# A hybrid decoder layer in fp32: the feed-forward products by one level of Strassen, with block sums kept in DRAM

## The chip, the core and the metric

The kernel runs on one core of a Trainium2 chip. The core has TensorE (matmul), VectorE, ScalarE, GpSimd and SyncE, each with its own instruction queue taken in order, an on-chip memory (SBUF) of 128 partitions, eight PSUM banks of 128 x 512 fp32 that TensorE writes, and 16 DMA engines that move data from and to DRAM. The metric is the device time of one execution in microseconds, as the median of several runs.

## What is computed

One decoder layer for 1024 tokens with 1024 channels: a modulated RMS norm, one input projection into gated DeltaNet heads and sliding-window attention heads, an output projection with a gated residual, then a second modulated norm and a SwiGLU feed-forward part, again with a gated residual. All of it is fp32. The change concerns the feed-forward part:

```python
D_FF = ((8 * D_MODEL // 3 + 255) // 256) * 256        # 2816
...
h2 = rms_norm(x, norm2_w[l]) * (1.0 + scale2) + shift2
ffn = (jax.nn.silu(h2 @ w_gate[l]) * (h2 @ w_up[l])) @ w_down[l]
x = x + gate2 * ffn
```

## The kernel before

Activations lie with channels on the partitions and tokens along the row: `h2` is eight blocks of 128 channels, `x1` the residual in eight blocks, each in two halves (`hf`) of 512 tokens. A matmul takes a 128x128 block of weights and 512 tokens. TensorE multiplies operands of reduced width in one pass, so each fp32 operand is split into a high and a low part (`split`: ScalarE copies the high part, GpSimd or VectorE subtracts to get the low one), and each product takes three passes, high x high, high x low and low x high (`mm3`). A unit (`unit`) is the three passes over all `KT` = 8 blocks of the inner dimension into one PSUM bank.

Weights come by `wunit`: a DMA of 512 KB on SyncE's queue into a raw tile, then `split` with GpSimd's subtraction. Pool `wp` holds two raw tiles and two split ones, so weights are prepared about one unit ahead.

The last stages are these. `out_proj(0)` and `out_proj(1)` multiply the mixed heads by `w_out`, one half of the tokens each, and update `x1` and a sum of squares. `norm2_gen(hf)` makes the row of reciprocal norms (a few matmuls, a chain of small VectorE steps in `rstd`, transposes in `rstd_row`) and then the modulated `h2` in high and low parts. The generator of the first half runs between the units of `out_proj(1)`, that of the second half between the first units of the feed-forward part.

The feed-forward part goes over the 22 blocks of 128 of the 2816 inner channels in four chunks (6, 6, 6, 4). For each block it runs four units (gate and up, two halves), takes SiLU from PSUM on ScalarE, multiplies on VectorE, and splits the result. After each chunk, eight output blocks by two halves are multiplied with `w_down` over the blocks of the chunk and added to `x1` from PSUM (line 1327). After the last chunk `x1` is stored.

The order of TensorE's instructions is that of the program text (`manual_schedule`). The order on the other engines, DMA issues on SyncE's queue included, is set ahead of time by a planner that takes instructions by their place in the text when they are ready on a timeline it works out. Tiles of one `tag` in a pool share `bufs` buffers; a new tile waits until the users of the buffer's last one are done. Tags that matter: `s16` in pool `p16` (four buffers of 16 KB a partition: `h`, `mixed`, then `act`), `s8` in `p8` (four of 8 KB), `scr` (three of 2 KB).

## Time and profile before

| | |
|---|---|
| runs | 1372.16 us median of 3 (1367.86 to 1377.49) |
| the profiled execution, its span | 1368.4 us |
| TensorE matmul busy | 1274.6 us, 93% of the span |
| VectorE, GpSimd, ScalarE busy | 653.0, 468.7, 436.1 us |
| moved by DMA | 144.12 MB, mean 105 GB/s |
| feed-forward part | from 641.8 us to the end |

Matmuls are pipelined, so the busy time of one overlaps that of the next, and the time from start to start is what counts. The shares are means over stages that differ much: in the first half of the span VectorE is busy most of the time, in the feed-forward part it is mostly idle. A wait is put down to the engine that released it last.

### The profile page before, as it was taken

What the parts mean: (1) busy time and instruction counts of PE and PEld (TensorE: products, weight loads), DVE (VectorE), ACT (ScalarE), POOL (GpSimd) and SP (SyncE); (2) the same over time, 40 slices, a digit from 0 to 9 for tenths busy, and PEclk for the clock granted to TensorE, in tenths of its full rate; (3) what the DMA queues carried; (4) which work ended last, traced back from release to release, by engine and by line L of the source; (5) the groups of instructions that cost most, each with busy time, mean ns of one, the idle gap of its engine ahead of it and who ended that gap; (6) DMA issues with size and microseconds to landing.
All of it is one profiled execution on the core that took longest, in us unless ns stands there. A gap on an engine that the chain in (4) does not pass through costs nothing.

```text
span 1368.4 us, 18093 instructions
## 1 busy us (share of the span) xinstructions
PE 1274.6 (93%) x7106; PEld 1053.8 (77%) x7106; DVE 653.0 (48%) x1315; ACT 436.1 (32%) x787; POOL 468.7 (34%) x295
## 2 busy tenths in 40 slices
PE   6878697896999999999999999999999999999998
PEld 5767576684787777777788888888888888888887
DVE  7989899889425776666611211212211221211122
ACT  3464454422426775334411101112101211111210
POOL 5566445435333443455312122222222221222221
PEclk7878898998998999999999999999999999999999
DMA  8627378483758764323111111111111111111113
GB/s 325 220 83 273 122 165 237 131 257 104 217 154 148 139 131 134 101 87 101 46 45 43 35 46 62 47 47 54 35 53 59 46 46 44 44 59 56 39 60 117
DMA packets 111620, 144.12 MB, mean 105 GB/s; under 512 B 36528, under 2 KB 77744, under 8 KB 111408
## 3 DMA queue, kind: packets, MB, share of 16 engines
q1 hardware_dynamic: 101936, 134.58, 32.1%
q0 software_dynamic: 9600, 8.39, 3.7%
...
HBM read 118.14 MB, written 24.77 MB: 104 GB/s over the span
## 4 chain that ended last, share of the span: by engine, by line
PE 53%; ACT 1%; DVE 1%; POOL 0%; issue 0%; POOLq 0%; ACTq 0%
PE ps_d L203 6%; PE ps_d L202 6%; PE ps_d L201 6%; PE ps_u L201 6%; PE ps_u L203 6%; PE ps_u L202 6%; PE ps_g L202 6%; PE ps_g L203 6%; PE ps_g L201 6%; PE ps_o L203 0%; PE ps_o L202 0%; PE ps_o L201 0%; DVE xn L319 0%; DVE h L321 0%; ACT w_o L181 0%; POOL xn L323 0%
## 5 line engine op out<-in xcount | busy, mean ns | idle before, releaser
L1319 DVE TENSOR_TENSOR av<-ps_u,av 128x512 f32<-128x512 f32 x44 | 30.4, 692 | 333.4 <-PE ps_u L203 330.2
L201 PE MATMUL ps_d<-act,w_d 128*128 128x512 f32 x352 | 136.9, 389 | 0.0
L202 PE MATMUL ps_d<-act,w_d 128*128 128x512 f32 x352 | 136.9, 389 | 0.0
L203 PE MATMUL ps_d<-act,w_d 128*128 128x512 f32 x352 | 136.9, 389 | 0.0
L1327 DVE SCALAR_TENSOR_TENSOR x<-ps_d,modc,x 128x512 f32<-128x512 f32 x64 | 48.1, 751 | 181.6 <-PE ps_d L203 181.5
L1318 ACT ACTIVATE av<-ps_g 128x512 f32<-128x512 f32 x44 | 26.2, 598 | 181.3 <-PE ps_g L203 181.2
L182 DVE TENSOR_TENSOR act<-av,act 128x512 fp32r<-128x512 f32 x44 | 66.8, 1518 | 35.5 <-ACT act L181 35.5
L201 PEld LDWEIGHTS ps_d<-act,w_d 128*128 128x128 f32 x352 | 66.1, 188 | 13.7
L202 PEld LDWEIGHTS ps_d<-act,w_d 128*128 128x128 f32 x352 | 66.1, 188 | 13.7
L203 PEld LDWEIGHTS ps_d<-act,w_d 128*128 128x128 f32 x352 | 66.1, 188 | 13.7
L202 PE MATMUL ps_g<-h2l,w_g 128*128 128x512 f32 x168 | 65.6, 390 | 1.7 <-DVE h2l L326 1.7
L201 PE MATMUL ps_g<-h2h,w_g 128*128 128x512 f32 x168 | 65.5, 390 | 0.6 <-ACT h2h L324 0.6
L201 PE MATMUL ps_u<-h,w_u 128*128 128x512 f32 x168 | 65.5, 390 | 0.0
L203 PE MATMUL ps_g<-h2h,w_g 128*128 128x512 f32 x168 | 65.4, 389 | 0.0
L203 PE MATMUL ps_u<-h,w_u 128*128 128x512 f32 x168 | 65.4, 389 | 0.0
L202 PE MATMUL ps_u<-h,w_u 128*128 128x512 f32 x168 | 65.4, 389 | 0.0
L201 PE MATMUL ps_g<-h,w_g 128*128 128x512 f32 x168 | 65.4, 389 | 0.0
L202 PE MATMUL ps_g<-h,w_g 128*128 128x512 f32 x168 | 65.4, 389 | 0.0
L203 PE MATMUL ps_g<-h,w_g 128*128 128x512 f32 x168 | 65.4, 389 | 0.0
L201 PE MATMUL ps_u<-h2h,w_u 128*128 128x512 f32 x168 | 65.4, 389 | 0.0
L202 PE MATMUL ps_u<-h2l,w_u 128*128 128x512 f32 x168 | 65.4, 389 | 0.0
L203 PE MATMUL ps_u<-h2h,w_u 128*128 128x512 f32 x168 | 65.4, 389 | 0.0
...
## 6 DMA issues: line engine op xcount, KB each, us to landing
ada<-in_ada_dram SPq DMA_DIRECT2D x48, 512.0 KB, 5.3
xt<-in_xT_dram SPq DMA_DIRECT2D x16, 256.0 KB, 5.1
AQ<-aq SPq DMA_DIRECT2D x16, 256.0 KB, 4.1
KQ<-kq SPq DMA_DIRECT2D x4, 1024.0 KB, 6.3
kvq<-KQ SPq DMA_DIRECT2D x8, 512.0 KB, 5.6
aqb<-AQ SPq DMA_DIRECT2D x8, 512.0 KB, 6.0
qb<-QS POOLq DMA_DIRECT2D x16, 256.0 KB, 8.4
x<-in_xT_dram SPq DMA_DIRECT2D x16, 256.0 KB, 3.3
```

What stands on the lines that cost most here:

```text
L182: last = eng.tensor_tensor(out=r(lo), in0=src, in1=hi, op=ALU.subtract)
L201: pe.matmul(out, lhsT=r(lhs[0]), rhs=r(rhs[0]), start=first, stop=False)
L202: pe.matmul(out, lhsT=r(lhs[0]), rhs=r(rhs[1]), start=False, stop=False)
L203: pe.matmul(out, lhsT=r(lhs[1]), rhs=r(rhs[0]), start=False, stop=last)
L1318: act.activation(out=av, in_=pss[0, hf], func=AF.Silu)
L1319: dve.tensor_tensor(out=av, in0=pss[1, hf], in1=av, op=ALU.mult)
L1327: dve.scalar_tensor_tensor(out=x, in0=ps, scalar=modc[:, 40 + dt:41 + dt], in1=x, op0=ALU.mult, op1=ALU.add)
```

## The change

Gate, up and down products are each computed by one level of Strassen's method in Winograd's form. An operand is cut into 2 x 2 blocks; sums and differences of blocks (S1 to S4 of the weights, T1 to T4 of the activations) are formed, seven products of half size take the place of eight, and the results are added up (U2, U3 and so on). The 22 blocks of inner channels go in 11 pairs `p`; the halves are the even and the odd block of a pair, the first and second four channel blocks, and the first and second half of the tokens.

Sweep 1 runs over the pairs with two products (A11 B11 and A12 B21) for gate and up; the first is copied to DRAM (`XD`), and their sum gives the first quarter of the activations (`AD[:, p, 0]`). Sweep 2 runs over the pairs again with the other five products, adds them up with what `XD` holds, and stores six more blocks or block sums of the activations (`AD[:, p, 1:7]`). In two of the five, a bank that VectorE has read is accumulated on again by a later product. The down products follow, seven of them, each over all 11 pairs, with activations loaded from `AD` and split (`right`) and weights or weight sums loaded from DRAM and split (`left`), in the order P1, P2, P6, P7, P4, P5, P3; after each the results in PSUM update `x1`, through `U` where a sum serves two quarters. Sums of the down weights are formed ahead (`down_sums`) and kept in DRAM (`SD`). `x1` is stored to DRAM (`X1`) in `out_proj` and loaded again for the last stage. The pools lie on a stack: `w1` takes the place of `wp`; `wg2` and `ev` that of `w1` and `p8`; `sl`, `rw`, `wh` and `us` that of `p16`, `p4`, `wg2` and `ev`. Tiles without a tag and those of tag `e` move to a pool `px` (six and two buffers of 4 KB). The sums are in fp32 and are split into high and low parts after summing. The down weights lie in DRAM by quarters. Comments and docstrings go. Cut to its core:

```diff
+    px = ctx.enter_context(tc.tile_pool(name="px", bufs=6))
+    def open_pool(name, bufs):
+        stack.append(tc.alloc_tile_pool(name=name, bufs=bufs, reuse_waits="tile"))
+    p16 = open_pool("p16", 4)
+    p4 = open_pool("p4", 2)
+    p8 = open_pool("p8", 4)
+    wp = open_pool("wp", 2)
...
+            if dt % 2:
+                sp.dma_start(out=X1[dt // 2, hf], in_=x1p[dt // 2, hf])
...
-            modulate(hi, lo, t2(f"xn2_{hf}{k}"), x1(k, hf), row, a, sh, (dve, pool)[k % 2])
+    def first_half():
+        for i, k in enumerate((0, 1, 2, 3, 4, 5, 6, 7)):
+            if k % 2 == 0:
+                b8 = p8.tile([P, 2, 2, TH], F32, tag="s8", name=f"B1_{k}")
+            B1[k], f1[k] = (b8[:, k % 2, 0], b8[:, k % 2, 1]), x1(k, 0)
+            modulated(f1[k], k, 0, (dve, pool)[k % 2])
+            split(B1[k][0], B1[k][1], f1[k], dve)
+    def second_half():
+        for n in ("T2", "T3", "T1", "T4"):
+            t = p16.tile([P, 4, 2, TH], F32, tag="s16", name=n)
...
+        for i in range(4):
...
+            modulated(b12, i, 1, pool)
+            modulated(b22, i + 4, 1, pool)
+            dve.tensor_tensor(out=b3, in0=b22, in1=b12, op=ALU.subtract)
+            dve.tensor_tensor(out=b12, in0=b12, in1=b11, op=ALU.subtract)
+            dve.tensor_tensor(out=b11, in0=b22, in1=b12, op=ALU.subtract)
+            dve.tensor_tensor(out=b21, in0=b21, in1=b11, op=ALU.subtract)
+            for n, src in (("T2", b11), ("T3", b3), ("T1", b12), ("T4", b21), ("B22", b22)):
+                split(T_[n, i][0], T_[n, i][1], src, dve)
...
+    close_pools(1)
+    w1 = open_pool("w1", 4)
+    def weights1(p):
+        for j in range(2):
+            raw = w1.tile([P, KT, P], F32, tag="r", name=f"r{j}_{p}", bufs=2)
+            sp.dma_start(out=raw, in_=SRC[j][2 * p])
+            for a in range(2):
+                w = w1.tile([P, 2, 4, P], F32, tag="w", name=f"w{j}{a}_{p}", bufs=4)
+                split(w[:, 0], w[:, 1], raw[:, 4 * a:4 * a + 4], pool)
...
+    def down_sums(d, k0, k1):
+        t = p16.tile([P, 4, 4, P], F32, tag="s16", name=f"sd{d}_{k0}")
+        sp.dma_start(out=t[:, :, 0:n], in_=wdown[d][:, :, k0:k1])
+        dve.tensor_tensor(out=a22, in0=a21, in1=a22, op=ALU.add)
+        dve.tensor_tensor(out=a21, in0=a11, in1=a21, op=ALU.subtract)
+        dve.tensor_tensor(out=a11, in0=a22, in1=a11, op=ALU.subtract)
+        dve.tensor_tensor(out=a12, in0=a12, in1=a11, op=ALU.subtract)
+        sp.dma_start(out=SD[d][:, :, k0:k1], in_=t[:, :, 0:n])
+    for d in range(4):
+        for k0 in (0, 4, 8):
+            down_sums(d, k0, min(k0 + 4, NP))
+    for p in range(NP):
+        w = weights1(p)
+        for a in range(2):
+            for j in range(2):
...
+                mm_block(ps[j], lambda i: (w[j, a][:, 0, i], w[j, a][:, 1, i]), lambda i: B1[4 * a + i], 4, a == 0)
+                if a == 0:
+                    x = t2(f"X{j}_{p}")
+                    act.activation(out=x, in_=ps[j], func=AF.Copy)
+                    sp.dma_start(out=XD[p, j], in_=x)
+                next(n2, None)
+        av = t2(f"av{p}")
+        act.activation(out=av, in_=ps[0], func=AF.Silu)
+        dve.tensor_tensor(out=av, in0=ps[1], in1=av, op=ALU.mult)
+        sp.dma_start(out=AD[:, p, 0], in_=av)
+        if p == 0:
+            second_half()
+    close_pools(2)
+    wg2 = open_pool("wg2", 10)
+    ev = open_pool("ev", 1)
+    def weights2(p, j):
+        wa, wb, ws = (px.tile([P, 2, 4, P], F32, tag="s4", name=f"w{x}{j}_{p}") for x in "abs")
+        sp.dma_start(out=wa.rearrange("p a k n -> p (a k) n"), in_=SRC[j][2 * p])
+        sp.dma_start(out=wb.rearrange("p a k n -> p (a k) n"), in_=SRC[j][2 * p + 1])
+        a11, a12, a21, a22, s1 = wa[:, 0], wa[:, 1], wb[:, 0], wb[:, 1], ws[:, 0]
+        dve.tensor_tensor(out=s1, in0=a21, in1=a22, op=ALU.add)
+        dve.tensor_tensor(out=a21, in0=a11, in1=a21, op=ALU.subtract)
+        dve.tensor_tensor(out=a11, in0=s1, in1=a11, op=ALU.subtract)
+        dve.tensor_tensor(out=a12, in0=a12, in1=a11, op=ALU.subtract)
+        for n, src in (("S2", a11), ("S3", a21), ("S1", s1), ("A22", a22), ("S4", a12)):
+            w = wg2.tile([P, 2, 4, P], F32, tag="w", name=f"w{n}{j}_{p}")
+            split(w[:, 0], w[:, 1], src, pool)
...
+    for p in range(NP):
+        ops = ev.tile([P, 6, TH], F32, tag="ops", name=f"ops{p}")
+        sg = ev.tile([P, 3, TH], F32, tag="sg", name=f"sg{p}")
+        for j in range(2):
+            w = weights2(p, j)
...
+            sp.dma_start(out=u2, in_=XD[p, j])
+            product(p6, "S2", "T2", True)
+            dve.tensor_tensor(out=u2, in0=p6, in1=u2, op=ALU.add)
+            product(p7, "S3", "T3", True)
+            dve.tensor_tensor(out=u3, in0=p7, in1=u2, op=ALU.add)
+            product(p5, "S1", "T1", True)
+            dve.tensor_tensor(out=c22, in0=p5, in1=u3, op=ALU.add)
+            product(p7, "A22", "T4", False)
+            dve.tensor_tensor(out=c21, in0=p7, in1=u2, op=ALU.add)
+            product(p5, "S4", "B22", False)
+            dve.tensor_tensor(out=c12, in0=p5, in1=u2, op=ALU.add)
+            if j == 0:
+                for c in (c22, c21, c12):
+                    act.activation(out=c, in_=c, func=AF.Silu)
             else:
+                for i, c in enumerate((c22, c21, c12)):
+                    dve.tensor_tensor(out=c, in0=c, in1=sg[:, i], op=ALU.mult)
+        sp.dma_start(out=b11, in_=AD[:, p, 0])
+        dve.tensor_tensor(out=t3_, in0=b22, in1=b12, op=ALU.subtract)
+        dve.tensor_tensor(out=t1_, in0=b12, in1=b11, op=ALU.subtract)
+        dve.tensor_tensor(out=t2_, in0=b22, in1=t1_, op=ALU.subtract)
+        dve.tensor_tensor(out=t4_, in0=b21, in1=t2_, op=ALU.subtract)
+        sp.dma_start(out=AD[:, p, 1:7], in_=ops)
+    close_pools(4)
+    sl = open_pool("sl", 22)
+    rw = open_pool("rw", 2)
+    wh = open_pool("wh", 3)
+    us = open_pool("us", 1)
+    def right(n):
+        for i in range(NP):
+            t = sl.tile([P, 2, TH], F32, tag="t", name=f"t{n}_{i}")
+            raw = us.tile([P, TH], F32, tag="tr", name=f"t{n}_{i}r", bufs=4)
+            sp.dma_start(out=raw, in_=AD[:, i, n])
+            split(t[:, 0], t[:, 1], raw, dve)
+    def left(src, name):
+        raw = rw.tile([P, NP, P], F32, tag="r", name=f"r{name}")
+        w = wh.tile([P, 2, NP, P], F32, tag="w", name=f"w{name}")
+        sp.dma_start(out=raw, in_=src)
+        split(w[:, 0], w[:, 1], raw, pool)
+    U = [us.tile([P, TH], F32, name=f"U{d}") for d in range(4)]
+    def last(name, t, src, key, first, after):
+        rhs = right(t)
+        for d in range(4):
+            w = left(src(d), f"{name}{d}")
...
+            mm_block(banks[key, d], w, lambda i: rhs[i], NP, first)
+            after(d, banks[key, d])
+    last("P1", 0, lambda d: wdown[d][:, 0], 1, True, lambda d, ps: act.activation(out=U[d], in_=ps, func=AF.Copy))
...
+    last("P2", 1, lambda d: wdown[d][:, 1], 1, False, after_p2)
...
+    last("P6", 4, lambda d: SD[d][:, 0], 6, True, after_p6)
+    last("P7", 5, lambda d: SD[d][:, 2], 7, True, after_p7)
+    last("P4", 6, lambda d: wdown[d][:, 3], 7, False, after_p4)
+    last("P5", 3, lambda d: SD[d][:, 3], 5, True, after_p5)
+    last("P3", 2, lambda d: SD[d][:, 1], 5, False, after_p3)
```

## Rows read from the trace of the kernel before

**Rows 1.** The table of windows: us, busy us of each engine (xinstructions), PEclk, DMA share, GB/s

```profile
core 0: us, PE busy (x) PEld busy (x) DVE busy (x) ACT busy (x) POOL busy (x), PEclk, DMA share, GB/s
0.00:34.00 34.00, 21.35 (x117) 18.62 (x118) 25.78 (x42) 13.31 (x20) 17.16 (x30) 0.79 0.90 327
600.00:642.00 42.00, 40.14 (x177) 32.53 (x177) 29.54 (x25) 20.21 (x27) 24.82 (x11) 1.00 0.25 79
642.00:1368.40 726.40, 720.35 (x3180) 595.56 (x3179) 164.42 (x178) 131.52 (x178) 163.87 (x79) 1.00 0.17 52
666.00:673.00 7.00, 4.78 (x20) 3.07 (x18) 4.03 (x6) 6.11 (x8) 1.73 (x2) 1.00 0.00 0
```

**Rows 2.** Timeline of TensorE and VectorE: start us, us, engine, line, operation

```profile
641.83 0.39 PE L201 MATMUL ps_g<-h,w_g 128*128 128x512 f32 x1
...
706.45 0.69 DVE L1319 TENSOR_TENSOR av<-ps_u,av 128x512 f32<-128x512 f32 x1 [14.24 <-PE ps_u L203]
...
728.21 0.69 DVE L1319 TENSOR_TENSOR av<-ps_u,av 128x512 f32<-128x512 f32 x1 [12.26 <-PE ps_u L203]
...
1364.61 0.75 DVE L1327 SCALAR_TENSOR_TENSOR x<-ps_d,modc,x 128x512 f32<-128x512 f32 x1 [1.97 <-PE ps_d L203]
```

**Rows 3.** Timeline of VectorE, GpSimd and ScalarE in the feed-forward part

```profile
707.83 0.69 DVE L182 TENSOR_TENSOR act<-av,act 128x512 fp32r<-128x512 f32 x1 [0.70 <-ACT act L181]
713.48 2.47 DVE L182 TENSOR_TENSOR act<-av,act 128x512 fp32r<-128x512 f32 x1 [0.97 <-ACT act L181]
...
713.00 2.40 POOL L182 TENSOR_TENSOR w_u<-w_u3r,w_u 128x1024 fp32r<-128x1024 f32 x1 [8.00 <-ACT w_u L181]
...
1321.85 1.30 POOL L182 TENSOR_TENSOR w_d<-w_d31r,w_d 128x512 fp32r<-128x512 f32 x1 [9.10 <-ACT w_d L181]
...
711.86 1.06 ACT L181 ACTIVATE w_u<-w_u3r 128x1024 fp32r<-128x1024 f32 x1 [4.06 <-PE ps_u L203]
712.83 0.62 ACT L181 ACTIVATE act<-av 128x512 fp32r<-128x512 f32 x1
```

**Rows 4.** Line 1327, the PSUM-fed update: duration ns min/median/max, first and last start

```profile
L1327 DVE SCALAR_TENSOR_TENSOR x<-ps_d,modc,x x64: 750/751/752, 781.2 to 1364.6; 128x512 f32<-128x512 f32 x64
```

**Rows 5.** Timeline of SyncE's queue, ScalarE and VectorE where the feed-forward part begins

```profile
628.61 0.33 SPq L193 DMA_DIRECT2D w_g0r<-in_wgate_dram  x1
...
636.64 1.06 ACT L181 ACTIVATE w_g<-w_g0r 128x1024 fp32r<-128x1024 f32 x1 [3.86 <-PE ps_o L203]
...
642.04 0.75 DVE L1199 SCALAR_TENSOR_TENSOR x<-ps_o,modc,x 128x512 f32<-128x512 f32 x1 [1.30 <-PE ps_o L203]
643.70 2.48 DVE L1206 TENSOR_TENSOR ssum<-ssum,sqx 128x512 f32<-128x512 f32 x1 [0.91 <-ACT sqx L1205]
648.26 0.16 DVE L266 TENSOR_SCALAR ms_n<-ssps 128x4 f32<-128x4 f32 x1 [2.08 <-PE ssps L1215]
...
650.24 2.40 DVE L175 SCALAR_TENSOR_TENSOR rs_n<-rsq_n 128x4 f32<-128x4 f32 x1
```

**Rows 6.** DMA issues: queue, count, KB each, median us from issue to landing

```profile
KQ<-kq SPq DMA_DIRECT2D x4, 1024.0 KB, 6.3
...
x<-in_xT_dram SPq DMA_DIRECT2D x16, 256.0 KB, 3.3
out_dram<-x SPq DMA_DIRECT2D x16, 256.0 KB, 2.0
...
w_g1r<-in_wgate_dram SPq DMA_DIRECT2D x1, 512.0 KB, 3.4
```

**Rows 7.** Windows around an idle stretch of TensorE, columns as in rows 1

```profile
147.00:160.00 13.00, 0.77 (x4) 0.35 (x3) 13.00 (x36) 5.83 (x9) 2.34 (x1) 0.73 0.34 121
160.00:164.00 4.00, 4.00 (x14) 3.33 (x15) 1.43 (x8) 2.64 (x6) 0.00 (x0) 0.61 0.02 4
164.00:168.00 4.00, 4.00 (x22) 3.26 (x21) 3.75 (x6) 1.46 (x3) 2.40 (x1) 1.00 0.11 33
```

167 lines of the change are left out of this document (106 added, 61 removed).

## Prediction

> **What bounds the kernel now.** I read the page's table of slices first, then a table of windows over the end of the kernel. The reader is to see that from about 640 us to the end TensorE is busy all the time at full granted clock, while VectorE, ScalarE and GpSimd are each busy about a fifth of it [rows 1]. The feed-forward part runs from the first gate matmul at 641.83 to the last `x` update at 1364.61, 722.8 us, and it is one long stream of 128x512 matmuls. Their pitch is read from two `av` products one block of 96 matmuls apart: (728.21 - 706.45) / 96 = 0.2267 us [rows 2]; the 0.39 us that a row gives for one matmul overlaps its neighbours. Before there are 22 x 2 x 2 x 8 x 3 = 2112 matmuls for gate and up and 8 x 2 x 22 x 3 = 1056 for down, 3168 x 0.2267 = 718.2 us. The other 4.6 us are the small matmuls of the norm and a wait of 2.2 us between 666 and 673 (4.78 us busy of 7), where the second half of `h2` comes late [rows 1].
>
> **What is removed.** Seven products for eight: 2772 matmuls of the same shape, 396 fewer, 396 x 0.2267 = **-89.8 us** if TensorE stays fed. The wait at 666 to 673 goes too, since the second half of the tokens is no longer needed until sweep 2: -2.2. Everything else in the change is a cost that TensorE either hides or doesn't. By stage TensorE needs 528 x 0.2267 = 119.7 us (sweep 1), 1320 x 0.2267 = 299.2 us (sweep 2, 27.2 for each `p`) and 924 x 0.2267 = 209.5 us (the down products).
>
> **Prices of the added work.** A VectorE operation on 128x512 takes 0.69 us; a GpSimd subtraction 1.30 us for 512 and 2.40 us for 1024 columns; a ScalarE copy 0.62 us for 512 and 1.06 us for 1024 [rows 3]. Two rows together say more: the VectorE subtraction with both inputs in SBUF takes 0.69 us alone but 2.47 us at 713.48, while a GpSimd subtraction that began at 713.00 runs to 715.40. VectorE ends 0.55 us after it, so the two run one behind the other. The PSUM-fed update takes 0.75 us in all 64 cases, next to GpSimd or not [rows 4]. So I count "SBUF pairs" on VectorE and all GpSimd work as one resource, and PSUM-fed VectorE work apart.
>
> **SyncE's queue.** All loads and stores stand in one queue. The stores of `SD`, `XD`, `AD` and `X1` wait there for VectorE or ScalarE, and weight loads behind them wait too. A raw tile is asked for about one `p` (10.9 us) ahead of its matmuls in sweep 1 and one (p, j) (13.6 us) ahead in sweep 2, and takes 3.4 us to land [rows 6]. A store late by less than the difference costs nothing, which I take; more lateness is in the upper ends below.
>
> **Output projection.** Eight more stores of 512 KB, and the first block sums of the down weights, which can start in the `s16` buffers that free there. VectorE is busy 29.5 of 42 us and the DMA share is 0.25 [rows 1]; the sums can get in front of an `x` or `ssum` step in VectorE's queue. Between 0 and 6, I take **+2**.
>
> **Start of sweep 1.** Pool `w1` reuses `wp`. Before, ScalarE splits `w_g0` at 636.64, five us before it is needed, because it takes the buffer of the last but one projection unit [rows 5]. Now either the raw tiles or the first hi/lo tiles lie on the buffer of the last one, which ends at 641.8. At best only copy and subtraction are late (0.62 + 1.30 = 1.9); at worst the load too (3.4 us for 512 KB [rows 6], 0.33 to issue [rows 5]: 5.7 in all, 7 with `ssum`'s late end). I take the worse, **+5**: the raw tiles are the first tag of the pool. After that the norm's row is asked for after a block of 12 matmuls, 2.72 us, where it had 24; the chain from 648.26 to the end of its last step at 652.64 [rows 5] is longer: **+1**.
>
> **Within sweep 1.** Steady state hides: for each `p` (10.9 us of TensorE) ScalarE has 7 operations, about 4.3 us, GpSimd 4 x 1.30 = 5.2 us. But the block sums (12 tiles x 4) and the second half of the tokens (4 x 9) add 84 SBUF pairs, 84 x 0.69 = 58.0 us, to GpSimd's (44 + 8) x 1.30 = 67.6: 125.6 us on one resource in 119.7, unless some of it runs before. The copies of `X` wait in ScalarE's queue behind copies that wait for VectorE, and the second product into the same bank waits for `X`. Between 0 (all early) and 20 (two periods of lag), **+6**, the excess of the two sums.
>
> **Sweep 1 to 2.** The new weight tiles lie on `B1` and `w1`; the first of them can be free 5.4 us early (nothing lost), or at the end (0.62 + 1.30, and a second subtraction: 4). **+2**.
>
> **Sweep 2.** For each `p`: VectorE 8 weight sums, 3 products, 4 block sums (15 SBUF pairs, 10.4 us) and 10 PSUM-fed adds (6.9 us); GpSimd 10 x 1.30 = 13.0; ScalarE 13 x 0.62 = 8.1. The shared resource has 23.4 of 27.2 us, VectorE alone 17.3: both fit. If VectorE never overlaps GpSimd it is 30.3, 3.1 over, 11 x 3.1 = 34 us. Two adds of each (p, j) are urgent: the banks `p7` and `p5` are read and then accumulated on again one product (2.72 us) later; after its 0.69 us an add has 2.0 us to spare, about one SBUF pair behind one GpSimd operation (0.69 + 1.30). New weights are split as buffers come free, one after each product, so one such pair in front of an urgent add is usual and two are rare: between 0 and 34, **+8** (0.36 for each of the 22).
>
> **Sweep 2 to down products.** This is the largest loss I can place. The last `ops` must be stored before its SBUF region becomes the raw buffers of `right`. After the last matmul: last add, its product and four block sums, 6 x 0.69 = 4.1 us; a store of 1.5 MB, by the rows for stores of 256 KB (2.0) and 1024 KB (6.3) on one line 2.0 + 4.3 x 1280/768 = 9.2 us [rows 6]; a load of 256 KB, 3.3 us; ScalarE's copy 0.62; issues 0.7: about 18 us with TensorE idle. Then eleven right tiles come through four raw buffers, each 3.3 + 0.62 + 0.69 = 4.6 us round, one in 1.15 us where TensorE uses one in 0.68: 11 x 1.15 - 7.5 = about 5. Before, after 13 us in which TensorE was busy for 0.8, the granted clock was 0.61 for 4 us and then full [rows 7]: most of the 4 us at the lower level (1.2 of 2.4 GHz), which loses about 2 us; I add 1 of them, as the tiles are late anyway. **+24**. If the raw buffers lie on memory that is free earlier it is about 5; with GpSimd's 1408-column subtractions (2.40 x 1408/1024 = 3.3 us) in VectorE's way, 32.
>
> **Down products.** For each, TensorE has 29.9 us; VectorE 11 subtractions (7.6) plus 4 to 12 updates of 0.75, GpSimd 4 x 3.3 = 13.2: at most 29.8 on the most loaded one. TensorE hides it; the two sides' loads are 20.2 + 20.2 MB in 209.5 us, 193 GB/s. +0. The end is as before.
>
> **Sum.** -89.8 - 2.2 + 2 + 5 + 1 + 6 + 2 + 8 + 24 = -44.0. The profiled execution spans 1368.4; the median of the runs, 1372.16, lies 3.8 above it, which I keep. 1368.4 - 44.0 + 3.8 = **1328 us**. With all costs at their low ends 1372.2 - 92.0 + 1.9 + 5 = 1287, with all at their high ends (6 + 7 + 1 + 20 + 4 + 34 + 32 = 104) 1384.
>
> **Rivals.**
> 1. *No gap before the down products.* The raw buffers lie on memory free earlier. For: I can't see addresses in the trace. 24 becomes 5: **1309**. Chance 0.12.
> 2. *DMA is the bound in sweep 1.* Its bytes: gate and up 11.5 MB, down weights in and out 23.1, `X` 5.8, `av` 2.9: 43.3 MB, where the feed-forward part moved 52 GB/s. The highest rate in the trace is 327 GB/s in the first 34 us [rows 1]; at that it takes 132.4 us, 12.7 above TensorE. In place of the 6: **1335**. Against: part of the sums runs ahead. Chance 0.08. The Trainium skill, "DMA: Bandwidth & Descriptors", section "Specifications", sets a limit of about 358 GB/s from HBM for one core; by that, as an estimate, 121 us, 1.2 above TensorE, and the trace's 327 lies below it.
> 3. *VectorE is the bound in sweep 2*, held by GpSimd all the time: 34 in place of 8, **1354**. For: [rows 3]. Against: the PSUM-fed adds don't wait. Chance 0.15.
> 4. *Slower: the urgent adds stand behind the weight sums.* Each engine takes its queue in order. If k of the four sums of the next weights stand in front of one urgent add in each (p, j), each held by a GpSimd operation, the add is late by 1.99k + 0.69 - 2.72. k = 2 costs 1.95 x 22 = 43 (1363), k = 3 3.94 x 22 = 87, in place of 8: **1407**. From three sums on it decides. Against: the sums are ready long before, so the planner can place them in idle time. Chance 0.13.
>
> **How the numbers follow.** The forecast as summed has 0.52. A measurement of this kernel tells changes of about 1%, so faster means below 1358.4. Forecast (less 0.03 for its upper tail), rivals 1 and 2, and half of rival 3 are faster: 0.49 + 0.12 + 0.08 + 0.07 = 0.76, given as 0.75; within 1%: the other half of rival 3 and that tail, 0.11; slower: rival 4 and a remainder, 0.14. The range takes in rivals 1 to 3, leaves out rival 4 and the ends: 1302 to 1368. Nearly all of it has one sign.
>
> **What would show it.** Matmuls of the feed-forward part 2772 at 0.227 us. An idle stretch of TensorE of some 18 us, once, ended by a DMA of `right`'s raw tile and ScalarE's copy, with a lower granted clock behind it: if it is missing, rival 1. In sweep 2 about 27.5 to 28 us for each `p`; waits of TensorE for the adds into `u3` and `c22` under 10 us in total; above 30 us for each `p` with VectorE busy throughout, rival 3; with VectorE part idle and TensorE waiting for those adds, rival 4. In sweep 1 a DMA rate near 327 GB/s with weight loads late is rival 2. The forecast is wrong if TensorE's idle time from 640 us on exceeds 80 us.

## The result and the profile after

The changed kernel takes 1390.5 us (median of 4 runs, 1385.0 to 1393.0) against 1372.7 for the kernel before; the ratio is 1.0131, 95% interval 1.0091 to 1.0171. It is slower by 1.3%, where 1328 was predicted, in a range of 1302 to 1368. Its profiled execution spans 1391.3 us.

TensorE has its 2772 matmuls, 396 fewer, so 89.8 us less to do, and the time went up all the same. The first place to look is the windows, with the columns of [rows 1]:

```profile
core 0: us, PE busy (x) PEld busy (x) DVE busy (x) ACT busy (x) POOL busy (x), PEclk, DMA share, GB/s
600.00:620.00 20.00, 16.40 (x57) 12.94 (x56) 16.30 (x25) 8.67 (x13) 8.74 (x5) 0.74 0.79 290
620.00:640.00 20.00, 18.99 (x83) 15.08 (x81) 19.83 (x21) 9.50 (x15) 9.89 (x4) 1.00 0.65 219
640.00:660.00 20.00, 12.94 (x46) 9.54 (x46) 12.46 (x20) 2.84 (x4) 2.70 (x2) 0.89 0.94 323
660.00:680.00 20.00, 12.74 (x45) 9.77 (x46) 8.75 (x24) 4.97 (x9) 7.16 (x6) 0.68 1.04 393
680.00:700.00 20.00, 12.25 (x41) 9.17 (x39) 16.49 (x16) 12.81 (x20) 15.84 (x11) 0.74 0.51 188
700.00:720.00 20.00, 15.45 (x55) 12.19 (x56) 19.77 (x28) 11.65 (x22) 14.39 (x5) 0.83 0.72 229
720.00:820.00 100.00, 99.72 (x440) 82.06 (x439) 19.98 (x23) 37.82 (x68) 51.57 (x40) 1.00 0.52 175
...
811.10:1149.70 338.60, 309.86 (x1321) 249.50 (x1319) 222.92 (x262) 87.05 (x142) 156.11 (x110) 0.98 0.42 144
```

Before, TensorE was busy for 40.14 of 42 us up to 642 and for 720.35 of the 726.4 behind it [rows 1]. Now 600 to 720 has five stretches with 12 to 16 of 20 us, at a granted clock of 0.68 to 0.89. From 720 to 820, the rest of sweep 1 and the first 9 us of sweep 2, nothing is lost. In sweep 2 (the last row) TensorE is idle for 28.7 of 338.6 us. Which operation ended the idle time is in the groups of instructions (busy us, mean ns of one | idle before, and what ended it):

```profile
L1353 PE MATMUL ps_c<-B,w 128*128 128x512 f32 x176 | 72.6, 413 | 15.4 <-ACT w L192 9.7 <-ACT X L1397 5.7
L1355 PE MATMUL ps_c<-B,w 128*128 128x512 f32 x176 | 72.2, 410 | 6.7 <-POOL w L193 6.6
L1353 PE MATMUL ps<-T,wA 128*128 128x512 f32 x88 | 37.7, 428 | 26.0 <-DVE xu L1448 25.1 <-ACT wS L192 0.8
L1353 PE MATMUL ps_P<-t,wP 128*128 128x512 f32 x308 | 121.4, 394 | 21.3 <-ACT t L192 21.3
```

`ps_c` is sweep 1: waits for the first weights (9.7), for a copy of `X` (5.7) and for weight splits (6.6). `ps<-T,wA` is the product `A22 T4` of sweep 2, which waits for the add into `u3` (L1448) 25.1 us in all, 16 times. `ps_P` is the gap before the down products.

From the first and last matmul of each group of tiles come the stages, here for every kernel that ran (us; sweep 1 is counted to the first matmul of sweep 2; "gap" is TensorE's idle time before the first down product; need is matmuls x 0.2267, the pitch of [rows 2]). no_sums and t_paced leave work out. The kernels from no_sums to pools were run once each, and the four runs of the changed kernel differ by 8 us, so for these a few us of the total say nothing; the stages of the profiled execution do.

| kernel | time | output projection ends | to first gate matmul | sweep 1 | sweep 2 | gap | down products |
|---|---|---|---|---|---|---|---|
| need | | 642.0 (before) | 0 | 119.7 | 299.2 | 0 | 209.5 |
| changed kernel | 1390.5 | 655.3 | 9.7 | 146.1 | 338.6 | 20.8 | 216.8 |
| no_sums | 1369.8 | 642.5 | 5.3 | 141.7 | 337.3 | 20.9 | 216.3 |
| t_paced | 1357.4 | 647.8 | 4.9 | 123.4 | 337.4 | 20.9 | 217.3 |
| spread | 1406.7 | 649.6 | 5.4 | 164.5 | 344.1 | 20.9 | 216.4 |
| order2 | 1382.0 | 650.5 | 10.7 | 146.3 | 330.6 | 20.8 | 217.4 |
| order3 | 1353.2 | 652.6 | 10.2 | 145.5 | 301.2 | 20.9 | 216.7 |
| dve_split | 1360.2 | 649.2 | 10.4 | 147.5 | 308.8 | 21.1 | 217.4 |
| pools | 1388.1 | 654.8 | 9.5 | 146.2 | 338.8 | 13.2 | 219.8 |
| best1 | 1318.3 | 644.0 | 2.1 | 124.6 | 310.9 | 15.7 | 216.2 |
| best2 | 1319.8 | 643.2 | 2.1 | 127.1 | 313.4 | 0.7 | 227.3 |
| best3 | 1316.0 | 643.3 | 2.1 | 141.4 | 308.4 | 0 | 216.1 |
| best4 | 1295.3 | 640.4 | 2.1 | 125.3 | 305.8 | 0 | 216.1 |

The stages that no edit touched repeat within 2 us (the sweep 2 of spread apart), except the end of the output projection. That one carries what the stages before it took in each run: the first `out_proj` matmul starts between 498.9 and 508.4. From the middle of the output projection (the first matmul of `out_proj(1)`) to its end are 51.0 us before, 60.1 to 63.3 in the five kernels that have the down sums there, and 49.5 to 51.2 in the other seven. Over need, the changed kernel loses 13.3 + 9.7 + 26.4 + 39.4 + 20.8 + 7.3 = 116.9 us, where the prediction counted 48.

### The profile page after: what moved, and what is told of

It is laid out like the page before. It is cut to its first block, busy times and chain, and to the rows that moved or that the text cites. A ratio compares the mean times of both kernels' runs of the same rounds, so it can differ in the third digit from the quotient of the medians.

```text
span 1391.3 us, 18693 instructions
## 1 busy us (share of the span) xinstructions
PE 1214.1 (87%) x6710; PEld 990.9 (71%) x6710; DVE 914.7 (66%) x1634; ACT 541.0 (39%) x972; POOL 630.3 (45%) x405
## 4 chain that ended last, share of the span: by engine, by line
PE 46%; DVE 14%; DMA 10%; issue 4%; POOL 4%; ACT 2%; SPq 0%; DVEq 0%; POOLq 0%; ACTq 0%
PE ps_P L1355 5%; PE ps_P L1354 5%; PE ps_P L1353 5%; PE ps L1353 3%; PE ps L1354 3%; PE ps L1355 3%; DMA wb<-in_wgate_dram 3%; PE ps_c L1353 3%; PE ps_c L1355 3%; PE ps_c L1354 3%; POOL wA L193 2%; DMA wb<-in_wup_dram 2%; DMA qb<-QS 1%; DVE wb L1418 1%; PE ps_gz L212 1%
## 5 line engine op out<-in xcount | busy, mean ns | idle before, releaser
L193 POOL TENSOR_TENSOR wP<-rP,wP 128x1408 fp32r<-128x1408 f32 x28 | 92.6, 3308 | 152.4 <-ACT wP L192 127.8
L1353 PE MATMUL ps_P<-t,wP 128*128 128x512 f32 x308 | 121.4, 394 | 21.3 <-ACT t L192 21.3
L1354 PE MATMUL ps_P<-t,wP 128*128 128x512 f32 x308 | 121.4, 394 | 1.9 <-DVE t L193 1.9
L1355 PE MATMUL ps_P<-t,wP 128*128 128x512 f32 x308 | 120.8, 392 | 0.0
L1355 PE MATMUL ps<-T,wS 128*128 128x512 f32 x264 | 102.8, 389 | 0.3 <-POOL wS L193 0.3
L1354 PE MATMUL ps<-T,wS 128*128 128x512 f32 x264 | 102.7, 389 | 0.0
L1353 PE MATMUL ps<-T,wS 128*128 128x512 f32 x264 | 102.7, 389 | 0.0
L193 POOL TENSOR_TENSOR w<-r,w 128x512 fp32r<-128x512 f32 x44 | 68.4, 1565 | 66.7 <-ACT w L192 65.6
L193 POOL TENSOR_TENSOR wS<-wa,wS 128x512 fp32r<-128x512 f32 x44 | 60.5, 1376 | 60.1 <-ACT wS L192 47.3
L1353 PE MATMUL ps_c<-B,w 128*128 128x512 f32 x176 | 72.6, 413 | 15.4 <-ACT w L192 9.7
L1353 PEld LDWEIGHTS ps_P<-t,wP 128*128 128x128 f32 x308 | 58.5, 190 | 34.6 <-ACT t L192 22.5
L1355 PE MATMUL ps_c<-B,w 128*128 128x512 f32 x176 | 72.2, 410 | 6.7 <-POOL w L193 6.6
L192 ACT ACTIVATE wP<-rP 128x1408 fp32r<-128x1408 f32 x28 | 38.5, 1376 | 88.0 <-DMA rP<-in_wdown_dram 33.8
L1354 PE MATMUL ps_c<-B,w 128*128 128x512 f32 x176 | 71.6, 407 | 0.0
L1354 PEld LDWEIGHTS ps_P<-t,wP 128*128 128x128 f32 x308 | 58.5, 190 | 16.1 <-DVE t L193 3.8
L1355 PEld LDWEIGHTS ps_P<-t,wP 128*128 128x128 f32 x308 | 58.4, 190 | 12.1
L1353 PE MATMUL ps<-T,wA 128*128 128x512 f32 x88 | 37.7, 428 | 26.0 <-DVE xu L1448 25.1
L193 POOL TENSOR_TENSOR wA<-wb,wA 128x512 fp32r<-128x512 f32 x22 | 33.3, 1514 | 59.3 <-DVE sg L1453 26.4
L256 POOL TENSOR_TENSOR ada<-ada,cb 128x1024 f32<-128x1024 f32 x17 | 44.8, 2657 | 27.8 <-DMA ada<-in_ada_dram 14.2
L1355 PEld LDWEIGHTS ps<-T,wS 128*128 128x128 f32 x264 | 49.5, 188 | 10.9 <-POOL wS L193 0.7
L1353 PEld LDWEIGHTS ps<-T,wS 128*128 128x128 f32 x264 | 49.6, 188 | 10.3
L1354 PEld LDWEIGHTS ps<-T,wS 128*128 128x128 f32 x264 | 49.5, 188 | 10.3
```

The lines of the kernel that those rows point to most:

```text
L192: act.activation(out=r(hi), in_=src, func=AF.Copy)
L193: last = eng.tensor_tensor(out=r(lo), in0=src, in1=hi, op=ALU.subtract)
L256: eng.tensor_tensor(out=w, in0=w, in1=cb, op=ALU.mult)
L1353: pe.matmul(ps, lhsT=r(wh), rhs=r(xh), start=first and i == 0, stop=False, **kw)
L1354: pe.matmul(ps, lhsT=r(wh), rhs=r(xl), start=False, stop=False, **kw)
L1355: pe.matmul(ps, lhsT=r(wl), rhs=r(xh), start=False, stop=i == n - 1, **kw)
```

## The experiments

The theory that was tested, Q: the time is lost because work that nobody needs soon stands ahead of urgent work in a queue that is taken in order (VectorE's, ScalarE's, GpSimd's, SyncE's). Its rival, R: it is the amount of work on VectorE and GpSimd, which share a resource, wherever that work stands.

### Sweep 1 and what is ahead of it: no_sums, t_paced, spread

no_sums takes out the loop that calls `down_sums`, and reads plain blocks for sums:

```diff
-    for d in range(4):
-        for k0 in (0, 4, 8):
-            down_sums(d, k0, min(k0 + 4, NP))
```

> The block sums of the down weights (12 tiles, 48 VectorE operations, 23.1 MB of loads and stores) are left out; the four of the seven down products that take a sum from DRAM take a plain block of the same size instead. Everything else is as in the changed kernel. Theory Q (these sums stand in VectorE's and SyncE's queues ahead of the norm's chain and of the first weight loads): the output projection ends 10 us sooner (about 645 instead of 655), the first gate matmul comes within 4 us of it instead of 10, sweep 1 takes at most 126 us instead of 146.1; in all 30 to 45 us off 1391 (1346 to 1361). Rival (the pool that takes the last projection's memory, and the second half of the tokens at the first p, cause it): the start stays at 660 or later and sweep 1 at 135 or more; at most 18 us off. Sweep 2 (338) and the gap behind it (21) stay in both.

Half of it came: 1369.8, 20.7 us less. The output projection ends at 642.5 again (51.2 us from its middle instead of 61.7) and the first gate matmul comes at 647.8 instead of 665.0. But sweep 1 itself still took 141.7 us. TensorE's waits there, by its timeline:

```profile
647.82 0.79 PE L1353 MATMUL ps_c<-B,w 128*128 128x512 f32 x1 [5.35 <-ACT w L192]
...
672.17 0.80 PE L1355 MATMUL ps_c<-B,w 128*128 128x512 f32 x1 [5.84 <-POOL w L193]
681.98 0.79 PE L1353 MATMUL ps_c<-B,w 128*128 128x512 f32 x1 [5.62 <-ACT X L1394]
```

and GpSimd ahead of the wait that ends at 672.17:

```profile
659.12 11.32 POOL L1241 TENSOR_TENSOR x<-x,row_n 128x512 f32<-128x512 f32 x8
670.40 5.11 POOL L193 TENSOR_TENSOR w<-r,w 128x512 fp32r<-128x512 f32 x3
```

The eight multiplications of the second half of the tokens (11.32 us) stand in one block ahead of the weight splits that the second p needs. That work is for sweep 2, 130 us later. So t_paced takes no_sums and lets it come in eight pieces:

```diff
-        if p == 0:
-            second_half()
+        if 1 <= p < 1 + 8:
+            with tc.issue_after(done["X"].ins), tc.issue_after(done["av"].ins), tc.issue_after(done["pool"].ins):
+                second_half(p - 1)
```

The edit also advances the norm's generator at every second block of sweep 1 only, and gives the T tiles another order.

> As no_sums (the block sums of the down weights left out, plain blocks in their place), and the second half of the tokens comes in eight pieces, one for each p from p=1 to 8, each behind that p's copy of X on ScalarE, behind its av product on VectorE and behind the weight splits on GpSimd; before all of it came as soon as it could. The same operations as in no_sums. Theory Q (the second half of the tokens stands ahead of sweep 1's weight splits and copies of X in the queues): sweep 1 from 141.7 (no_sums) to 120 to 127 us, in all 1345 to 1356. Rival (the weights' loads and splits are too slow for the pace of sweep 1 as they are): sweep 1 stays at 135 or more, in all 1361 or more.

Sweep 1 fell to 123.4 us with the same operations, 3.7 over need, and the group of sweep 1 has no wait left but the first:

```profile
L1358 PE MATMUL ps_c<-B,w 128*128 128x512 f32 x176 | 69.5, 395 | 4.9 <-ACT w L192 4.9
```

The loads and splits of the weights are fast enough; their place was the cause. The total missed its expected range by 1.4 us; this run came to the output projection 5.4 us later than no_sums (506.7 against 501.3), in stages that neither edit touches.

spread keeps all sums, two tiles of up to 1 MB for each p from 0 to 5, inside sweep 1, and the second half of the tokens at p=6 in one block, both tied behind VectorE's `av` product:

```diff
+        with tc.issue_after(done["r"].ins):
+            for a in todo[2 * p:2 * p + 2]:
+                stores.append((down_load(*a), *a))
...
-        if p == 0:
-            second_half()
+        with tc.issue_after(done["av"].ins):
+            for a in stores:
+                down_sums(*a)
+            if p == 6:
+                second_half()
```

> The same sums, all of them, two tiles for each p from p=0 to 5, each load behind the raw weights of its p in SyncE's queue, each sum behind the av product of its p on VectorE, each store one p later behind the raw weights; the second half of the tokens at p=6 instead of p=0. Nothing is left out. Theory Q (the place in the queues costs the time, not the work): as without the sums, sweep 1 at most 126 us, start at most 650, in all 30 to 45 us off 1391. Rival R (125.6 us of VectorE pairs and GpSimd work on one shared resource in 119.7 us, which must all be inside sweep 1 now): the start improves but sweep 1 takes 130 us or more, at most 20 us off.

Neither theory had this: R's sweep of over 130 us came, but at 164.5 us, and the kernel got slower, 1406.7. Its windows, GpSimd, and the longest wait of TensorE in the first of them:

```profile
675.00:700.00 25.00, 17.62 (x60) 13.57 (x61) 14.60 (x17) 8.41 (x15) 11.08 (x8) 0.80 0.66 232
700.00:760.00 60.00, 55.49 (x234) 44.51 (x233) 30.56 (x40) 19.91 (x34) 27.18 (x20) 0.97 1.05 405
760.00:780.00 20.00, 10.44 (x33) 7.75 (x31) 19.42 (x31) 12.84 (x23) 12.94 (x2) 0.74 0.21 70
...
666.82 10.40 POOL L1241 TENSOR_TENSOR x<-x,row_n 128x512 f32<-128x512 f32 x8
...
678.96 0.79 PE L1355 MATMUL ps_c<-B,w 128*128 128x512 f32 x1 [6.04 <-POOL w L193]
```

From 700 to 760 the DMA engines move 405 GB/s at a share of 1.05, and a copy of `X` on ScalarE waits up to 8.05 us for an earlier store to `XD` to give its buffer back. That is what rival 2 of the prediction describes, made by putting the sums' 23 MB beside the weights of the first six p; but TensorE is idle for only 4.5 of those 60 us. More is lost on either side. At 760 to 780 VectorE's part of the second half of the tokens comes in one block, only later than before, and TensorE is busy for 10.44 of 20 us. And GpSimd's part never moved: the edit ties the block behind an instruction of VectorE alone, so the eight multiplications stand at 666.82 as in no_sums, ahead of the splits of the second p, and TensorE waits 6.04 us. So spread changed less than its expectation says, and does not decide between Q and R. Of the Trainium skill, the prediction gave "DMA: Bandwidth & Descriptors", "Specifications", with about 358 GB/s for one core. The trace disagrees: 405 over 60 us, reads and writes together. "HBM Reference", "Specifications (TRN2)", in the Trainium skill, says that a core streaming alone gets about 425, and with that this run agrees.

### Sweep 2: order2, order3, dve_split

VectorE around one of the waits of sweep 2, in the changed kernel (a set, below, is the work of one (p, j)):

```profile
971.08 1.75 DVE L1417 TENSOR_TENSOR ws<-wb 128x512 f32<-128x512 f32 x1 [0.25 <-DMA wb<-in_wup_dram]
972.75 0.68 DVE L1445 TENSOR_TENSOR xu<-ps,xu 128x512 f32<-128x512 f32 x1
973.35 0.68 DVE L1465 TENSOR_TENSOR ops<-b12d,b 128x512 f32<-128x512 f32 x1
973.95 1.78 DVE L1418 TENSOR_TENSOR wb<-wa,wb 128x512 f32<-128x512 f32 x1
975.65 0.68 DVE L1466 TENSOR_TENSOR ops<-ops 128x512 f32<-128x512 f32 x1
976.25 0.68 DVE L1419 TENSOR_TENSOR wa<-ws,wa 128x512 f32<-128x512 f32 x1
976.85 0.68 DVE L1448 TENSOR_TENSOR xu<-ps,xu 128x512 f32<-128x512 f32 x1
```

Three weight sums (L1417 to L1419) and two block sums (L1465, L1466) stand ahead of the add into `u3` (L1448), two of them held to 1.75 and 1.78 us by GpSimd; TensorE waits for it 2.05 us. Counting tells whose they are: this L1417 is the 14th of 22, the add the 11th, so the sums are those of the set three ahead. Nobody needs them for 40 us. In six of the 16 waits (9.2 of the 25.1 us) it is not the holding that makes the add late but a load. VectorE stands idle for 4.7 to 5.5 us in front of the first weight sum, with the adds behind it in its queue:

```profile
957.61 0.69 DVE L1417 TENSOR_TENSOR ws<-wb 128x512 f32<-128x512 f32 x1 [4.69 <-DMA wb<-in_wgate_dram]
958.22 0.69 DVE L1445 TENSOR_TENSOR xu<-ps,xu 128x512 f32<-128x512 f32 x1
```

The add into `u2` (L1445) starts 3.3 us after its product has ended, and the one into `u3` is late by it. order2 moves the four weight sums behind the add into `c22`, order3 the block sums too:

```diff
+        with ExitStack() as es:
+            if len(sets) >= 3:
+                es.enter_context(tc.issue_after(sets[-3].ins))
+            return weight_set(p, j)
...
-            dve.tensor_tensor(out=c22, in0=p5, in1=u3, op=ALU.add)
+            sets.append(dve.tensor_tensor(out=c22, in0=p5, in1=u3, op=ALU.add))
+            if late:
+                with tc.issue_after(sets[-1].ins):
+                    block_sums(*late.pop())
```

(the last three lines are order3's alone)

> Only the place of the four weight sums of sweep 2 in VectorE's queue: those of the set three ahead stand behind the add into c22 instead of behind u2, thus no longer ahead of the add into u3. The same operations and loads. Theory Q (the adds into u3 wait behind sums that nobody needs for 40 us): sweep 2 from 338.4 to 300 to 312 us, 26 to 38 off 1391, and TensorE's waits for that add (25.1 us in all, 16 times) nearly gone. Rival R (VectorE never overlaps GpSimd: 30.3 us of work for each p): sweep 2 stays at 333 or more, at most 5 us off.

Sweep 2 fell by 8 us only, to 330.6. Eight waits of 2.12 us were left, one for each p from 2 to 9, in the set where block sums were still ahead of `u3`:

```profile
964.15 0.68 DVE L1453 TENSOR_TENSOR xu<-ps,xu 128x512 f32<-128x512 f32 x1
964.75 1.48 DVE L1473 TENSOR_TENSOR ops<-b12d,b 128x512 f32<-128x512 f32 x1
966.27 0.69 DVE L1474 TENSOR_TENSOR ops<-ops 128x512 f32<-128x512 f32 x1
966.99 0.69 DVE L1475 TENSOR_TENSOR ops<-ops 128x512 f32<-128x512 f32 x1
967.60 0.68 DVE L1456 TENSOR_TENSOR xu<-ps,xu 128x512 f32<-128x512 f32 x1
```

The add into `u2` (L1453) comes 3.3 us after its product, behind two products by `sg` held to 1.77 and 1.82 us and the first block sum; then one operation held to 1.48 and two free ones are enough. I had moved half of what stood in the way.

> As order2, and the four block sums of each p (t3, t1, t2, t4) stand behind the add into c22 of the next p's first set too, with their store; before they stood between u2 and u3 of that set, where order2's trace shows one wait of 2.12 us for each p. The same operations. Theory Q (only the place of ready work ahead of the add into u3 costs time): sweep 2 from 338.6 (330.6 in order2) to 299 to 304 us, in all 1343 to 1352. Rival R (VectorE and GpSimd share one resource, 30.3 us for each p): sweep 2 stays over 325, in all 1370 or more.

Sweep 2 took 301.2 us, 2.0 over need, and the whole kernel 1353.2. The window of sweep 2:

```profile
808.30:1109.50 301.20, 299.98 (x1321) 247.41 (x1319) 235.94 (x262) 85.83 (x142) 157.86 (x110) 1.00 0.49 162
```

VectorE and GpSimd are busier than in the changed kernel (235.94 and 157.86 us against 222.92 and 156.11), with operations held as long (the L1418 of the changed kernel 1287 ns in the mean, here 1300), in 37 us less. So R does not hold: the amount of work fits. dve_split asks the same from the other side, by taking the holding away:

```diff
-            split(w[:, 0], w[:, 1], src, pool)
+            split(w[:, 0], w[:, 1], src, dve)
```

> The changed kernel with one edit: the low parts of sweep 2's weights are subtracted on VectorE instead of GpSimd, so that nothing of sweep 2 runs on GpSimd and no VectorE operation is held by it; VectorE then has 24 us of work in 27.2 for each p. Rival R (the sharing is what costs): the operations of 1.4 to 1.8 us fall to 0.69 and sweep 2 falls to 315 or less. Theory Q (what stands ahead of the add into u3 costs): five more operations for each set stand in the same queue, and sweep 2 stays within 10 us of 338 or gets longer.

Sweep 2 fell to 308.8, which is R's number, not Q's. The weight sums of VectorE, in the changed kernel first and then in dve_split (820 to 1130 us):

```profile
L1418 DVE TENSOR_TENSOR wb<-wa,wb 128x512 f32<-128x512 f32 x20 | 25.7, 1287 | 0.1
L1417 DVE TENSOR_TENSOR ws<-wb 128x512 f32<-128x512 f32 x20 | 21.0, 1052 | 41.5 <-DMA wb<-in_wgate_dram 38.7 <-DMA wb<-in_wup_dram 2.5
```

```profile
L1418 DVE TENSOR_TENSOR wb<-wa,wb 128x512 f32<-128x512 f32 x19 | 13.0, 686 | 0.3
L1417 DVE TENSOR_TENSOR ws<-wb 128x512 f32<-128x512 f32 x18 | 12.5, 692 | 17.7 <-DMA wb<-in_wup_dram 9.9 <-DMA wb<-in_wgate_dram 7.8
```

With GpSimd idle each sum takes 0.69 us, and what stands ahead of `u3` mostly fits its slack of 2.0 us: TensorE waits for it 5.8 us in place of 25.1. So the two runs together say: it takes work ahead of the urgent add, and something that draws this work out, GpSimd's holding or a late load. order3 takes away the first, dve_split much of the second, and Q alone, as I had it, was too simple. How much of dve_split's gain is the missing hold alone stays open: the rows show that VectorE's wait for `wb` fell too, from 41.5 to 17.7 us, and the queue's order moved a little (at 970 two sums stand ahead of `u3`, not three). "GPSIMD Engine Reference", "1. Specifications", in the Trainium skill, says that GpSimd's way to SBUF is shared with VectorE for operations with two inputs in SBUF; the 0.69 against 1.05 to 1.29 us agrees.

### The gap: pools

pools turns the order of the four pools of the down products round:

```diff
-    sl = open_pool("sl", 22)
+    us = open_pool("us", 1)
     rw = open_pool("rw", 2)
     wh = open_pool("wh", 3)
-    us = open_pool("us", 1)
+    sl = open_pool("sl", 22)
```

> Only the order in which the four pools of the down products are laid out in SBUF: raw right tiles and the left tiles first (on the T tiles, which are free one to four products before the end of sweep 2), the split right tiles last, so that no load waits for the store of the last ops. The same operations. Theory M (the raw tiles lie on ops): the gap of 21.0 us falls to 1 to 6, and the low clock behind it goes too, in all 15 to 26 us off 1391. Rival (the last block sums and the AD traffic hold the first right tiles anyway): the gap stays over 12, at most 9 us off.

The gap fell from 20.8 to 13.2; the time, 1388.1, lies among the runs of the changed kernel. The rival was nearer. In the changed kernel the chain through the gap is, on VectorE, GpSimd and SyncE's queue (the last two rows):

```profile
1154.52 0.69 DVE L1465 TENSOR_TENSOR ops<-b12d,b 128x512 f32<-128x512 f32 x1 [2.57 <-DMA b<-AD]
...
1155.97 3.53 DVE L1467 TENSOR_TENSOR ops<-ops 128x512 f32<-128x512 f32 x1
...
1155.40 7.11 POOL L193 TENSOR_TENSOR wP<-rP,wP 128x1408 fp32r<-128x1408 f32 x2 [30.81 <-ACT wP L192]
...
1159.53 0.32 SPq L1468 DMA_DIRECT2D AD<-ops  x1
...
1165.63 0.33 SPq L1489 DMA_DIRECT2D t_0r<-AD  x1
```

That is the prediction's chain: the last sums, the store (6.1 us until its memory is free), the load of the first right tile, its split. In pools the raw tiles had been asked for at 1143.9 and were there, but ScalarE copied three left tiles first, the third of which had to be loaded, and VectorE the block sums. One wait was taken away and the next one behind it ended last.

### Together: best1 to best4

best1 puts order3, the pieces of t_paced, another order of pools and the sums of the down weights, moved into sweep 2, into one kernel. Nothing is left out in any of the four. The sums' tiles in best1, and the raw weights of sweep 1 in halves:

```diff
-        t = p16.tile([P, 4, 4, P], F32, tag="s16", name=f"sd{d}_{k0}")
+        t = px.tile([P, 4, 2, P], F32, tag="s4", name=f"sd{d}_{k0}")
...
+            with tc.issue_after(sets[-1].ins):
+                while held:
+                    down_sums(*held.pop())
...
-            raw = w1.tile([P, KT, P], F32, tag="r", name=f"r{j}_{p}", bufs=2)
+                raw = w1.tile([P, 4, P], F32, tag="r", name=f"r{j}{a}_{p}", bufs=4)
```

> Everything computed, nothing left out. The queues put in order everywhere: as order3; the second half of the tokens as t_paced; the raw tiles of sweep 1 in halves, and laid out behind the split tiles; the block sums of the down weights moved into sweep 2, one tile of 512 KB for each set, behind c22; for the down products the pools ordered left raw, left, right raw (eleven buffers), right, on the memory that frees first, b11 asked for ahead of the last set. Theory Q: output projection to 642, first gate matmul within 3 us, sweep 1 122, sweep 2 300 to 306, gap 3 to 6, down products 210 to 213, end 4: 1283 to 1300 in all, ratio to before 0.935 to 0.95. Rival R: sweep 2 at 325 or more, for the 24 sums more: over 1315. Rival on DMA (sums in sweep 2 delay the weights): sweep 2 between 308 and 325 with TensorE waiting for weight tiles.

1318.3 us (ratio to before 0.9592, 0.9545 to 0.9639), faster than both kernels, but over the range of Q. Sweep 1 came near what was expected (124.6). Sweep 2, at 310.9, did not: TensorE waits 7.9 us for adds there, once 3.95 us, for an add that stood behind a weight sum whose load was late by 6.38. The gap was 15.7: the raw right tiles stood in SyncE's queue behind a store of down sums that waited for VectorE, and the raw left tile behind all of them, asked for at 1086.93, with the first matmul at 1097.31.

```diff
+                with tc.issue_after(done["t5"].ins):
+                    w = left(src(d), f"{name}{d}")
...
-                es.enter_context(tc.issue_after(sets[-3].ins))
+                es.enter_context(tc.issue_after(sets[-2].ins))
```

> As best1, everything computed, with four places in the queues changed. In sweep 2 the weight sums stand behind c22 of the set two ahead instead of three, so that a late load is not waited for in front of an urgent add (best1 waits 3.95, 1.87 and 0.74 us so), and the sums of the down weights end two sets earlier. At the gap SyncE asks for the first left tile first, then the right tiles, and ScalarE copies the other left tiles behind the sixth right tile; in best1 the raw right tiles stood behind a store that waited for VectorE, and the raw left tile, asked for at 1086.93, set the start at 1097.31. Theory Q: sweep 2 from 310.9 to 301 to 305 us, gap from 15.7 to 3 to 7, in all 1296 to 1306. Rival (the gap is the latency of loads behind the last products, whatever their order): gap over 10 and 1305 to 1315.

No gain: 1319.8 (0.9613, 0.9565 to 0.966). The first matmul came 0.7 us after the last, and then TensorE stopped at the next two tiles:

```profile
1091.78 0.80 PE L1359 MATMUL ps_P<-t,wP 128*128 128x512 f32 x1 [4.75 <-DVE t L193]
1102.74 0.80 PE L1358 MATMUL ps_P<-t,wP 128*128 128x512 f32 x1 [9.74 <-ACT t L192]
```

The wait had moved: VectorE did the block sums ahead of the first tile's low part, and the second right tile's buffer lay on `ops` and waited for its store. Two sets of lead for the weight sums were no better than three (313.4 against 310.9).

```diff
+                    whole = [t4(f"ops{p}_{i}", (P, 2, TH)) for i in range(3)]
...
+        if late:
+            with tc.issue_after(done["low"].ins), tc.issue_after(done["tr"].ins):
+                block_sums(*late.pop())
```

> Everything computed. Sweep 2's weight sums again three sets ahead, behind c22; the block sums of the down weights in 24 tiles of 512 KB on buffers that nothing else uses, 16 of them in sweep 1 (one or two for each p, behind that p's av product) and 8 in the first eight sets of sweep 2 (behind c22); so they take no buffer from the weights. For the last p the ops are held in three tiles that stay, and their four block sums and stores stand behind the splits of the first eleven right tiles; in best2 those sums stood ahead of the first right tile's low part (4.75 us), and the second right tile lay on ops and waited for their store (9.74 us). Theory Q: sweep 1 122 to 127, sweep 2 from 313.4 (best2) to 301 to 306, stall around the start of the down products from about 15 to at most 5, in all 1288 to 1303. Rival on DMA in sweep 1 (376 GB/s wanted, and spread was starved at 403 to 409): sweep 1 over 130. Rival R: sweep 2 over 310.

1316.0 (0.9587, 0.955 to 0.9624), outside the range again. The gap is gone; the down products need 216.1 and stall 5.1 us. But sweep 1 took 141.4, the number of the rival on DMA: the stores of the down sums stood ahead of the stores of `X`, and `ps_c` waited 10.0 us for copies of `X`. The DMA share was 0.69 to 0.93 there, so the engines were not full as in spread.

```diff
-            for _ in range(1 + p % 2):
-                down_load()
...
+            for _ in range(2 if len(sets) in (7, 9, 11, 13, 15, 17) else 2 <= len(sets) < 20):
+                down_load()
```

> Everything computed. As best3, but all 24 tiles of block sums of the down weights stand in sweep 2, from its third set on (one for a set, two in six of them), behind c22; in best3 their stores stood in SyncE's queue ahead of the stores of X in sweep 1, and ScalarE's copies of X waited for a scratch buffer (10.0 us of TensorE waits), and the weights of sweep 2's first sets were asked for late (5.34 us). Theory Q: sweep 1 from 140.2 to 122 to 126, sweep 2 from 308.4 to 301 to 305, the rest as best3: 1288 to 1300 in all, ratio 0.94 to 0.95. Rival R: with all the sums in sweep 2 VectorE's pairs and GpSimd no longer fit into 27.2 us for each p, sweep 2 over 310.

1295.3 us (5 runs, 1293.2 to 1302.6), ratio 0.9474, 0.9449 to 0.9499: 5.3% faster than before, and within the expected range. Its windows of sweep 1, sweep 2 and the start and rest of the down products:

```profile
640.00:768.00 128.00, 123.75 (x543) 101.48 (x542) 55.51 (x68) 63.62 (x109) 74.67 (x53) 0.99 0.60 195
768.00:1073.00 305.00, 301.10 (x1319) 246.52 (x1318) 259.56 (x358) 87.64 (x144) 158.79 (x111) 1.00 0.68 224
1073.00:1083.00 10.00, 7.58 (x25) 5.30 (x23) 8.25 (x11) 6.97 (x11) 3.23 (x1) 0.83 1.01 385
1083.00:1290.00 207.00, 205.13 (x902) 169.21 (x902) 101.40 (x110) 77.22 (x97) 86.06 (x26) 1.00 0.62 213
```

All the block sums of the down weights are in it, in sweep 2 alone, with VectorE busy for 259.56 of 305 us, and TensorE is still busy for 301.10. The work of the change fits under the matmuls; what stood in the way was its order in the queues and where its buffers lay.

## Why the prediction was wrong, point by point

What failed is the step from work to time: the work was added up for each engine, found to fit in the mean of a stage, and so priced at almost nothing, and the argument against rival 4 (ready early, so placed in idle time) did the rest. The runs showed that the order decides: the same operations in another order take 301.2 us instead of 338.6 in sweep 2. Four terms (output projection, start, sweep 1, sweep 2) came out above their own upper ends, and 1390 lies above the 1384 that the prediction gave with all costs at their high ends.

- **Removed matmuls**, -89.8, and the wait of -2.2: right. 2772 matmuls, and where nothing is late they run at the pitch of [rows 2]: the last `x` updates come 7.48 us apart, 33 matmuls each.
- **Output projection**, +2, bounds 0 to 6: 13.3, beyond the bound. 10.7 of it were lost from the middle of the projection on (61.7 us against 51.0), and that is the down sums; the other 2.6 this run had lost earlier, in stages that the change leaves alone. I had counted the down sums as a few operations in front of an `x` or `ssum` step. They took the chain of the first norm apart (its row came with a wait of 3.60 us), and 290 GB/s of loads and stores where before there were 79 [rows 1] stood in SyncE's queue. Without them, 51.2 us from the middle (no_sums).
- **Start of sweep 1**, +5 and +1: 9.7. Half is what I had, the buffer of the last projection unit (5.3 without the sums; 2.1 when raw and split tiles change places). The other half is the loads and stores of the down sums. The paragraph on **SyncE's queue** has them only as stores that hold back what stands behind them, and of that there was little: the first raw weights were asked for at 656.12, 0.8 us after the projection's last matmul, where no_sums asked 0.1 us after it. But their load took longer. In the changed kernel from 650 to 672, with the DMA engines at a share of 1.04 and 387 GB/s:

```profile
r<-in_wgate_dram SPq DMA_DIRECT2D x2, 512.0 KB, 9.5
```

In no_sums it took 4.0 us, and the prediction reckoned with 3.4 [rows 6]. The wait for the norm's row, +1 in the prediction, came as 2.14 us at 676 and is counted in sweep 1.
- **Within sweep 1**, +6, bounds 0 to 20: 26.4. The step that failed is that I added up work (125.6 us on one resource in 119.7) and asked whether it fits in the mean. It fits: 720 to 820 is perfectly fed, with VectorE busy for 20 of 100 us. But the second half of the tokens was all put at the front, ahead of weight splits and copies of `X`. TensorE is idle for 14.6 us of the sweep; of the rest, 7 us are 36 matmuls at the lower clock behind those waits, and 2.4 the norm's small matmuls. Without the down sums the sweep takes 141.7 (no_sums), with the second half in pieces as well 123.4 (t_paced), and with the down sums in sweep 2 it is 125.3 (best4).
- **Sweep 1 to 2**, +2: 0.
- **Sweep 2**, +8, bounds 0 to 34: 39.4. This is rival 4, given 0.13: k = 2 sums ahead of the urgent add, 43 us. It has the sign that the prediction named for it: over 30 us for each p (338.6 / 11 = 30.8), VectorE idle for a third of the time (222.92 us busy of 338.6), TensorE waiting for those adds (25.1 us). The step that failed is the argument against it, that "the sums are ready long before, so the planner can place them in idle time". The order of the queue was fixed when the program was built, and sums three sets ahead were put beside an urgent add. The rival has the weight sums alone; order2, which moves only these, gains 8 us, and the block sums were the other half. Nor does the rival have the loads: VectorE waited 41.5 us for `wb`, in six of the 16 waits straight ahead of a late add. My price of one held pair (1.99) was close; held sums took 1.2 to 1.8 us.
- **Sweep 2 to down products**, +24: 20.8 of gap and 7.3 more in the down products, 28.1. The chain was right step by step; its store took 6.1 us, not 9.2, and waits for `b` (2.57) and for GpSimd (3.53 for a sum of 0.69) made that up.
- **Down products**, +0: right behind their first 26 us, which belong to the term above.
- The sum in one line: 1368.4 - 92.0 + 116.9 = 1393.3, less 2.4 us of the norm's small matmuls, which the stages of sweep 1 count again: 1390.9, and 1391.3 was measured. Of the 69 us that the forecast lacked, the output projection and the two sweeps are 63 (11.3 + 20.4 + 31.4). Its falsifier, TensorE idle for more than 80 us from 640 on, was set badly: the idle time from 640 to 1387.3 was 78.6 us (668.67 busy of 747.3), since matmuls at the lower clock (a mean of 0.95 there) count as busy.
- Rival 1 did not happen in the changed kernel (a gap of 20.8). Rival 2 happened only where sweep 1 starts (393 GB/s and a share of 1.04 from 660 to 680, with the first weights late); in most of sweep 1 it is 175 GB/s. Rival 3's number (30.3 for each p) is near the 30.8 measured, but its mechanism fell with order3.
